# Two stretches of a kernel's own products, repeated behind its last store at other operand distances

## The chip, the cores and the metric

One core of a Trainium2 chip runs the kernel. The time is device microseconds of one execution; the metric is the median over runs.

## The reference

A two-layer decoder trunk on x of 512 tokens by 1024 features, float32, causal. Layer 0 mixes tokens by dilated sliding-window attention (three groups of eight heads, windows 128, 512 and 2048, dilations 1, 4 and 16, joined by their softmax denominators); layer 1 by a recurrent block (RG-LRU). Behind each stands a gated feed-forward part with a causal convolution. Each part is wrapped in two RMS norms and added to the stream:

```
for layer in range(2):
    h = rms_norm(x, norm_mix_pre[layer])
    h = dilated_attention(h) if layer == 0 else rglru(h)
    x = x + rms_norm(h, norm_mix_post[layer])
    h = rms_norm(x, norm_ffn_pre[layer])
    h = (gelu(conv(h @ w_up)[:, :3072]) * conv(h @ w_up)[:, 3072:]) @ w_down
    x = x + rms_norm(h, norm_ffn_post[layer])
```

## The kernel before

Each float32 operand of a large product is split into a high and a low part of type fp32r (`split`: ScalarE copies the high part, VectorE subtracts for the low part), and each product is three: high by high, high by low, low by high (`PASSES`, `mm3`). The moving operand has 512 columns ("long" here) or 256 ("short"); the stationary one has always 128 x 128.

The normed state is kept transposed in one tile, `hT`, high and low part, 2 x 8 x 512 numbers a partition. `new_hT(near)` allocates it with 16 spare numbers and starts the data at the first of them (`near`) or 64 bytes further on:

```
both = htp.tile([P, 2 * KD * S + NEAR], F32R, tag="hT", name=nm("hT"))
at = 0 if near else NEAR
```

In the built program the split weights (`whi`, `wlo`) start at 192 bytes past a multiple of 256, a near `hT` at 128, the other at 192. The state is near in the two feed-forward parts.

In nine of each twelve steps of the feed-forward's first product, and in the strided part of attention, the eight products of a 2 x 2 block scheme are replaced by seven (`seven`, `chain`, line 1040 in before): blocks of 256 columns, whose moving operand is a block of `hT`, or a sum of such blocks from tiles called `T` (`token_sums`), which stand partly on the same residue of 256 bytes as a near `hT` and partly on that of the weights. Between them stand long products: quarters of ordinary tiles, and the second product of the feed-forward (`rows`), both through `mm3` (line 411). In attention the value products (line 1238) stand between, with a weight as moving and `hT` as stationary operand.

The order of all work is written out by hand (the Tile framework's manual schedule), and each engine runs its instructions in that order; waits are set from what reads and writes the same tile. At the end, `norms` with `final` takes the last output tile through the post norm (`rms`, lines 418 to 427), adds it to the stream (line 583, VectorE) and stores it (line 585, queues of SP and ScalarE). `drain` lets what is left run out, and the program ends.

Of the kernel before, what the change touches and what calls it, by code (L numbers as in the profile page):

```python
# [11 lines left out]
F32 = mybir.dt.float32  # L12
# [32 lines left out]
APART, ROUND = 7, 44  # L45
QUARTERS = (28, 30, 31, 32, 34, 35, 36, 37, 38, 39, 40, 41, 42, 43, 45, 49)
HALF = ("s1", "w11", "w12", "a22", "s2", "s3", "s4", "rows", "act")

SHORT_ORDER = [
    ([0, 1], [0, 1, 2]), ([0], [3]), ([2, 3], [0]), ([1], [3]), ([2, 3], [1]), ([2], [2, 3]), ([3], [2, 3]),  # L50
# [33 lines left out]
def kernel(  # L84
# [25 lines left out]
    nc = tc.nc  # L110
# [24 lines left out]
    mm = nc.tensor.matmul  # L135
# [163 lines left out]
    def single(name):  # L299
        return (name[0] if isinstance(name, tuple) else name) in HALF  # L300

# [74 lines left out]
    def tick(length=1):  # L376
        for s in list(sides):
            s[0] -= length
            if s[0] <= 0:
                try:  # L380
                    s[0] = next(s[1])
                except StopIteration:
                    sides.remove(s)
        if not state["hold"]:
            pump(1 if state["even"] or state["live"] >= HALVES - 4 else 2)

    def drain():
        while sides:
            tick()
# [725 lines left out]
    def attention(hT, post, pre):  # L1115
# [50 lines left out]
        def first_values(vs):  # L1166
# [16 lines left out]

            ps = first_transposed(0, 0, range(2))
            warm(WARM - 2)
            take(ids[0], 0)
            first_split(0, 0, ps, range(2, 4))
# [452 lines left out]
    for layer in range(2):  # L1640
# [11 lines left out]
        for half, k in [(1, k) for k in range(0, TAIL, 4)] + [(0, REST[0])] + [(1, k) for k in range(TAIL, 24, 4)]:  # L1652
            rows = ffn_w_down[layer][k * P : (k + 4) * P, half * 512 : half * 512 + 512]
            plan.append(("value", 4, 512, [(rows.rearrange("(k p) c -> p k c", p=P), 512)]))

    def warm(n):

        for _ in range(n):
            mm(warm_ps, one[0][:, :P], one[0], start=True, stop=True)
# [44 lines left out]
    nc.vector.memset(one[0].bitcast(F32), 1.0)  # L1704
    warm_ps = psum("warm")
    warm(WARM)
    root_table()
    hT = attention(hT, (norm_mix_post, 0), (norm_ffn_pre, 0))
    hT = ffn(0, hT, (norm_ffn_post, 0), (norm_mix_pre, 1))
    hT = lru(hT, (norm_mix_post, 1), (norm_ffn_pre, 1))  # L1710
    ffn(1, hT, (norm_ffn_post, 1), None)
    drain()


_INS = [
# [24 lines left out]
```

## Time and profile before

| | |
|---|---|
| median of 2 runs | 1406.99 us (1406.71 to 1407.26) |
| the profiled execution, by its clock | 1406.83 us |
| its span, first to last instruction | 1405.1 us |
| TensorE products | 8741, busy 99% |
| weight loads on TensorE | 8741, busy 89% |
| VectorE, ScalarE, GpSimd busy | 80%, 56%, 16% |
| mean granted TensorE clock | 0.998 |

In the profile a matmul's duration holds the depth of its pipeline; the next one starts long before it ends. The view of windows gives for each stretch (us from the start of the span) its length, the busy time of each engine, the number of records in it, the granted clock, and the share and rate of the DMA engines; records that reach into a window are counted too. The timeline lists start, length, engine, line, operation and tiles, with what ended an idle time in brackets.

### The profile page before, as it was taken

The numbers are of one execution on the slowest core, as the hardware profiler recorded it, in microseconds if no ns is written. First come the engines' busy times: TensorE is split into PE (matmuls) and PEld (weight loads), VectorE is DVE, ScalarE is ACT, GpSimd is POOL, SyncE is SP. The second block draws the span as 40 slices with busy tenths as digits, with TensorE's granted clock in tenths as the row PEclk, the third lists the DMA queues.
The fourth block names the chain that finished last, engine by engine and source line by source line (L and its number), as shares of the span: only waits on it lengthen the run. The fifth ranks groups of instructions, "written<-read, shape, count | busy, mean of one in ns | idle before, by whom it ended". The sixth has DMA issues, their size and how long they took to land.

```text
span 1405.1 us, 23534 instructions
## 1 busy us (share of the span) xinstructions
PE 1395.4 (99%) x8741; PEld 1256.1 (89%) x8741; DVE 1122.2 (80%) x2201; ACT 791.2 (56%) x1646; POOL 225.5 (16%) x344
## 2 busy tenths in 40 slices
PE   9999999999999999999999999999999999999998
PEld 7888999999998898999999888888898999999886
DVE  6576897888866889998888758769789999888843
ACT  7343565454536556666665645589455666666641
POOL 0341342231310102221110001000101212111000
PEclk9999999999999999999999999999999999999999
DMA  7644464656564545766654632431444777664511
GB/s 229 178 141 120 121 182 139 188 149 179 152 213 145 197 157 106 162 153 163 131 138 104 215 130 91 135 121 60 131 145 93 165 150 165 150 136 121 179 54 60
DMA packets 171883, 201.92 MB, mean 144 GB/s; under 512 B 10560, under 2 KB 141080, under 8 KB 171512
## 3 DMA queue, kind: packets, MB, share of 16 engines
q1 hardware_dynamic: 123064, 153.34, 33.9%
q0 software_dynamic: 47856, 46.02, 18.0%
q8 instruction: 69, 1.13, 0.3%
q10 hardware_dynamic: 848, 1.05, 0.2%
q14 instruction: 46, 0.38, 0.1%
HBM read 181.41 MB, written 18.96 MB: 143 GB/s over the span
## 4 chain that ended last, share of the span: by engine, by line
PE 78%; ACT 4%; DVE 4%; issue 1%; DVEq 0%; ACTq 0%
PE ps L1040 34%; PE acc L411 25%; PE ps L411 11%; PE v L1238 6%; DVE xb L1543 1%; DVE wlo L149 1%; PE O L1450 1%; PE S L1384 1%; ACT whi L148 1%; ACT sig L1564 1%; PE tr L505 1%; ACT sig L1583 0%; ACT a L1581 0%; ACT xhi L148 0%; ACT th L1582 0%
## 5 line engine op out<-in xcount | busy, mean ns | idle before, releaser
L149 DVE TENSOR_TENSOR wlo<-raw,whi 128x512 fp32r<-128x512 f32 x620 | 408.8, 686 | 110.5 <-ACT whi L148 108.4
L148 ACT ACTIVATE whi<-raw 128x512 fp32r<-128x512 f32 x620 | 367.1, 625 | 150.8 <-PE acc L411 46.6
L1040 PE MATMUL ps<-T,whi 128*128 128x256 f32 x1664 | 300.6, 281 | 0.7 <-DVE ps L1058 0.7
L411 PE MATMUL ps<-hT,whi 128*128 128x512 f32 (+1 forms) x1088 | 287.6, 353 | 0.0
L1040 PEld LDWEIGHTS ps<-T,whi 128*128 128x128 f32 x1664 | 257.8, 189 | 5.3 <-DVE ps L1058 1.3
L1040 PE MATMUL ps<-T,wlo 128*128 128x256 f32 x832 | 232.9, 280 | 0.0
L1040 PE MATMUL ps<-hT,whi 128*128 128x256 f32 x1248 | 226.0, 280 | 0.0
L411 PEld LDWEIGHTS ps<-hT,whi 128*128 128x128 f32 x1088 | 189.6, 188 | 27.7
L1040 PEld LDWEIGHTS ps<-hT,whi 128*128 128x128 f32 x1248 | 192.9, 189 | 2.6
L411 PE MATMUL ps<-hT,wlo 128*128 128x512 f32 (+1 forms) x544 | 191.5, 352 | 0.0
L1040 PE MATMUL ps<-hT,wlo 128*128 128x256 f32 x624 | 174.7, 280 | 0.0
L185 POOL DMA_DIRECT2D raw<-in_ffn_w_up_dram x72 | 92.8, 1319 | 415.7 <-DVE wlo L149 291.6
L1040 PEld LDWEIGHTS ps<-T,wlo 128*128 128x128 f32 x832 | 158.2, 190 | 0.0
L411 PE MATMUL acc<-whi,ahi 128*128 128x512 f32 x352 | 137.6, 391 | 0.0
L411 PE MATMUL acc<-whi,alo 128*128 128x512 f32 x352 | 137.2, 390 | 0.2
L411 PE MATMUL acc<-wlo,ahi 128*128 128x512 f32 x352 | 137.0, 389 | 0.0
L1040 PEld LDWEIGHTS ps<-hT,wlo 128*128 128x128 f32 x624 | 118.8, 190 | 0.0
L411 PEld LDWEIGHTS ps<-hT,wlo 128*128 128x128 f32 x544 | 102.5, 188 | 14.5
L1049 ACT ACTIVATE part<-ps 128x256 f32<-128x256 f32 x156 | 59.1, 379 | 89.3 <-PE ps L1040 86.7
L1238 PE MATMUL v<-whi,hT 128*128 128x512 f32 x320 | 106.4, 396 | 0.0
L781 DVE SCALAR_TENSOR_TENSOR u<-ps,cols,u 128x511 f32<-128x511 f32 x120 | 89.5, 747 | 5.8 <-ACT u L777 3.7
L777 ACT ACTIVATE u<-ps,cols 128x512 f32<-128x512 f32 x60 | 46.3, 775 | 64.6 <-DVE ps L1053 50.1
(206 smaller groups left out, 2144.8 us busy)
## 6 DMA issues: line engine op xcount, KB each, us to landing
raw<-in_ffn_w_up_dram SPq DMA_DIRECT2D x48, 1024.0 KB
raw<-in_attn_w_qkv_dram SPq DMA_DIRECT2D x67, 512.0 KB
raw<-in_ffn_w_up_dram POOLq DMA_DIRECT2D x72, 256.0 KB, 4.8
raw<-in_ffn_w_down_dram SPq DMA_DIRECT2D x14, 1024.0 KB
dw<-in_ffn_w_down_dram SPq DMA_DIRECT2D x40, 256.0 KB
raw<-in_lru_w_in_dram SPq DMA_DIRECT2D x8, 1024.0 KB
turned<-T POOLq DMA_DIRECT2D x26, 256.0 KB, 2.6
ft<-turned POOLq DMA_DIRECT2D x104, 64.0 KB, 4.7
```

The lines of the kernel that those rows point to most:

```text
L148: nc.scalar.activation(hi, raw, AF.Copy)
L149: nc.vector.tensor_tensor(lo, raw, hi.bitcast(F32), op=ALU.subtract)
L185: nc.gpsimd.dma_start(to, src, accum_op=ALU.add)
L411: mm(dst, l[a], r[b], start=start and n == 0, stop=stop and n == 2)
L505: nc.tensor.transpose(ps[:, k * P : (k + 1) * P], xs[i][:, k * P : (k + 1) * P], ident)
L777: nc.scalar.activation(u, ps, AF.Identity, scale=own[:, j : j + 1], bias=cc[:, 48 + j : 49 + j])
L781: nc.vector.scalar_tensor_tensor(u[:, d:], ps[:, : S - d], wc, u[:, d:], op0=ALU.mult, op1=ALU.add)
L1040: mm(dst, W[wa][0][:, k, :], right[n](ha, k), start=n in (1, 5) and k == q == 0, stop=k == 3 and q == 2, skip_group_check=True,)
L1049: later(1, lambda: nc.scalar.activation(to, dst, AF.Copy))
L1238: mm(bank, hT[a][:, k, t * P : (t + 1) * P], W[b][k % 2][:, 0, :], start=(k, a, b) == (0, 0, 0), stop=(k, a, b) == (KD - 1, 1, 0),)
L1384: mm(ps[:, c], q[hh][:, c], k[hh][:, c], start=True, stop=True)
L1450: mm(po[:, c], vtile(v, r, 2 * gi + hh), pts[gi][:, r], start=gi == 0, stop=gi == 1)
```

## The change

A function `rows_again` is called behind `drain`. It allocates a state tile with `new_hT(True)` (the tile has one buffer, so its readers before must be done), fills the first half A with 1.0 on VectorE and the second half B on GpSimd, takes one PSUM bank, and issues products into it, each a sum of its own that nothing reads.

Two strings name the products. An element such as `sU4W31` is: s for 256 moving columns, l for 512; the moving operand's kind (T, H, U or W) and its slot of 512 numbers in A; the stationary operand's kind, slot in B and block of 128. `FFN_ROW` has 440 elements (368 s, 72 l) and `ATT_ROW` 410 (324 s, 86 l). Kind and size of the elements are in the same order as 440 products of a feed-forward part and 410 of attention (there with 64 products of 128 columns between them, left out here); H stands for `hT`, W for a weight, T and U for sums on the one and the other residue.

Each of the 64 entries of `VARIANTS` runs one string once: F for `FFN_ROW` (46 entries), A for `ATT_ROW` (18). Its three numbers move the operands of kind T, H and U by so many times 16 bytes; those of kind W stand at 12 such units. B starts 16,384 bytes behind A, so that the distance between the starts of two operands, modulo 256 bytes, is 16 times the difference of their numbers. The kernel's own distances are those of ("F", 8, 8, 12) and ("A", 8, 12, 12). The entries are: T = H = 0 to 15 with U at 12, then T = H = U = 0 to 15, then T at 8 and H at 0, 2, 4 ... (and the other way round), and 18 for `ATT_ROW`.

```diff
+VARIANTS = [
+    ("F", 0, 0, 12),
...
+    ("F", 15, 15, 12),
+    ("F", 0, 0, 0),
...
+    ("F", 15, 15, 15),
+    ("F", 8, 0, 12),
...
+    ("F", 0, 8, 12),
...
+    ("A", 8, 12, 12),
...
+    ("A", 13, 13, 13),
+]
...
+    def rows_again():
+
+        A, B = (h.rearrange("p k t -> p (k t)") for h in new_hT(True))
+        nc.vector.memset(A.bitcast(F32), 1.0)
+        nc.gpsimd.memset(B.bitcast(F32), 1.0)
+        ps = psum("again")
+        for kind, t, h, u in VARIANTS:
+            at = {"T": 4 * t, "H": 4 * h, "U": 4 * u, "W": 48}
+            for e in (FFN_ROW if kind == "F" else ATT_ROW).split():
+                n = 256 if e[0] == "s" else 512
+                mv = A[:, 512 * int(e[2]) + at[e[1]] :][:, :n]
+                st = B[:, 512 * int(e[4]) + 128 * int(e[5]) + at[e[3]] :][:, :128]
+                mm(ps[:, :n], st, mv, start=True, stop=True)
...
     ffn(1, hT, (norm_ffn_post, 1), None)
     drain()
+    rows_again()
```

TensorE at the seam, in the program of the change (`acc` is the last output tile's bank, `again` the new one, `hT` the new tile):

```order
L525 MATMUL acc_15331<-whi_15553,ahi_15628 128x512
L525 MATMUL acc_15331<-wlo_15554,ahi_15628 128x512
L525 MATMUL acc_15331<-whi_15553,alo_15629 128x512
L1782 MATMUL again_15888<-hT_15885 128x256 [waits DVE_49,Pool_49]
L1782 MATMUL again_15888<-hT_15885 128x256 x28
L1782 MATMUL again_15888<-hT_15885 128x512 x12
L1782 MATMUL again_15888<-hT_15885 128x256 x12
```

Before, the engine's program ended with the third row. The first added product waits for VectorE and GpSimd, the others for nothing.

VectorE's end in the program of the change (the last two operations on the stream, then the fill of A):

```order
L541 SCALAR_TENSOR_TENSOR s_15866<-s_15867,s_15866 128x1 [waits DVE_49]
L697 SCALAR_TENSOR_TENSOR x_sb_15316<-post_15861,s_15866,x_sb_15316 128x512 [waits DMAHW1_49,DVE_49]
L697 SCALAR_TENSOR_TENSOR x_sb_15316<-post_15862,s_15866,x_sb_15316 128x512
L1773 MEMSET hT_15885 128x4096
L1865 UNCONDITIONAL_BRANCH
```

Before, the branch stood right behind the stream's last operation. The lines above `rows_again` are 114 further down than in the kernel before (583 is 697).

GpSimd's end in the program of the change (its last weight loads, then the fill of B):

```order
L299 DMA raw_14433<-in_ffn_w_up_dram 128x4x128 [waits DVE_49]
L299 DMA raw_14621<-in_ffn_w_up_dram 128x4x128 [waits DMAHW3_49,DMASW6_49,DMASW3_49]
L299 DMA raw_14621<-in_ffn_w_up_dram 128x4x128 [waits DVE_49]
L1774 MEMSET hT_15885 128x4096 [waits PE_49]
L1865 UNCONDITIONAL_BRANCH
```

Before, the branch stood behind the last load. The fill waits for TensorE's last product that reads the tile's earlier content.

More of the change, by code (lines that the diff above doesn't have):

```diff
@@ L47 @@
 HALF = ("s1", "w11", "w12", "a22", "s2", "s3", "s4", "rows", "act")
+FFN_ROW = (
[22 rows of a table added]
+)
+ATT_ROW = (
[21 rows of a table added]
+)
+VARIANTS = [
+    ("F", 0, 0, 12),
+    ("F", 1, 1, 12),
+    ("F", 2, 2, 12),
+    ("F", 3, 3, 12),
+    ("F", 4, 4, 12),
+    ("F", 5, 5, 12),
+    ("F", 6, 6, 12),
+    ("F", 7, 7, 12),
+    ("F", 8, 8, 12),
+    ("F", 9, 9, 12),
+    ("F", 10, 10, 12),
+    ("F", 11, 11, 12),
+    ("F", 12, 12, 12),
+    ("F", 13, 13, 12),
+    ("F", 14, 14, 12),
+    ("F", 15, 15, 12),
+    ("F", 0, 0, 0),
+    ("F", 1, 1, 1),
+    ("F", 2, 2, 2),
+    ("F", 3, 3, 3),
+    ("F", 4, 4, 4),
+    ("F", 5, 5, 5),
+    ("F", 6, 6, 6),
+    ("F", 7, 7, 7),
+    ("F", 8, 8, 8),
+    ("F", 9, 9, 9),
+    ("F", 10, 10, 10),
+    ("F", 11, 11, 11),
+    ("F", 12, 12, 12),
+    ("F", 13, 13, 13),
+    ("F", 14, 14, 14),
+    ("F", 15, 15, 15),
+    ("F", 8, 0, 12),
+    ("F", 8, 2, 12),
+    ("F", 8, 4, 12),
+    ("F", 8, 6, 12),
+    ("F", 8, 10, 12),
+    ("F", 8, 12, 12),
+    ("F", 8, 14, 12),
+    ("F", 0, 8, 12),
+    ("F", 2, 8, 12),
+    ("F", 4, 8, 12),
+    ("F", 6, 8, 12),
+    ("F", 10, 8, 12),
+    ("F", 12, 8, 12),
+    ("F", 14, 8, 12),
+    ("A", 8, 12, 12),
+    ("A", 0, 12, 12),
+    ("A", 4, 12, 12),
+    ("A", 5, 12, 12),
+    ("A", 7, 12, 12),
+    ("A", 9, 12, 12),
+    ("A", 11, 12, 12),
+    ("A", 13, 12, 12),
+    ("A", 8, 8, 12),
+    ("A", 8, 0, 12),
+    ("A", 8, 4, 12),
+    ("A", 8, 11, 12),
+    ("A", 8, 13, 12),
+    ("A", 8, 8, 8),
+    ("A", 0, 0, 0),
+    ("A", 4, 4, 4),
+    ("A", 11, 11, 11),
+    ("A", 13, 13, 13),
+]
 SHORT_ORDER = [
```

43 rows, old and new, of tables (ATT_ROW, FFN_ROW) are left out of this document.

## The prediction

> **What bounds the kernel now.** I read the page first: busy shares, granted clock, the chain that ended last.
>
> ```profile
> span 1405.1 us, 23534 instructions
> PE 1395.4 (99%) x8741; PEld 1256.1 (89%) x8741; DVE 1122.2 (80%) x2201; ACT 791.2 (56%) x1646; POOL 225.5 (16%) x344
> PEclk9999999999999999999999999999999999999999
> PE 78%; ACT 4%; DVE 4%; issue 1%; DVEq 0%; ACTq 0%
> ```
>
> TensorE never rests in 1405 us: 8741 products, full clock. The reader is to see that a product added to this engine has nothing to hide beside. What one costs is its distance to the start of the next, not the "mean ns of one", which includes the pipeline (a 256-column product is listed with 280 ns while another starts each 120 ns). So I take stretches of one kind, and divide their length by the products that start in them. The view of windows gives length and count; the count includes the one to four products that reach in from before.
>
> ```profile
> 498.27:511.97 13.70, 13.70 (x124) 1.00 0.42 149
> 875.64:890.11 14.47, 14.47 (x123) 1.00 0.27 86
> 545.56:553.73 8.17, 8.17 (x74) 1.00 0.53 66
> 511.97:545.56 33.59, 33.59 (x146) 1.00 0.47 114
> 1321.76:1397.84 76.08, 76.08 (x337) 1.00 0.23 83
> ```
>
> Rows one to three are "short" products (256 columns): 120, 120 and 72 start there, so 114.2, 120.6 and 113.5 ns each. Rows four and five are "long" ones (512 columns): 144 and 335, so 233.3 and 227.1 ns. What differs inside a kind is the place of the operands. I took the addresses from the two programs and give the **distance** as start of the moving operand minus start of the stationary one, modulo 256 bytes, where a row of 16-byte units has 16 values. Rows one, three and four have distance 192 (the state that was allocated "near"), rows two and five distance 0. So a distance costs a short product up to 7 ns, in the other order a long one 6 ns. No other distance occurs among such products in this trace; that is the gap of this forecast.
>
> The two stretches that the change repeats stand in this trace too. The string FFN_ROW is the 440 products from 560.03 us on (again at 1094.20), ATT_ROW those from 300.13 on without 64 small products of 128 columns, 16 of which are in the last row here:
>
> ```profile
> 560.03:619.42 59.39, 59.39 (x442) 1.00 0.73 158
> 1094.20:1153.59 59.39, 59.39 (x443) 1.00 0.74 158
> 300.13:365.22 65.09, 65.09 (x475) 1.00 0.61 169
> 334.82:336.52 1.70, 1.70 (x19) 1.00 1.01 323
> ```
>
> FFN_ROW: 59.39 us, twice the same to 0.01. ATT_ROW: 65.09 - 64 x 1.70/16 = 58.3 us.
>
> **The change part by part.** Nothing is removed. Added are one fill on VectorE, one on GpSimd, and on TensorE 46 x 440 + 18 x 410 = 27,620 products with as many weight loads: counted by kind, 22,760 short and 4,860 long.
>
> *The fills and the seam.* The end of the trace, TensorE and VectorE, and the clock:
>
> ```profile
> 1397.84 0.39 PE L411 MATMUL acc<-whi,alo 128*128 128x512 f32 x1
> 1400.30 1.41 DVE L583 SCALAR_TENSOR_TENSOR x_sb<-post,s,x_sb 128x512 f32<-128x512 f32 x2
> 1399.00:1400.00 1.00, 0.00 (x0) 0.00 (x0) 0.96 (x4) 0.28 (x1) 0.00 (x0) 1.00 0.00 0
> 1400.00:1401.00 1.00, 0.00 (x0) 0.00 (x0) 0.93 (x4) 0.00 (x0) 0.00 (x0) 0.88 0.00 0
> 1401.00:1402.00 1.00, 0.00 (x0) 0.00 (x0) 0.71 (x2) 0.00 (x0) 0.00 (x0) 0.50 0.07 27
> L1704 DVE MEMSET one<- x1: 485/485/485, 0.9 to 0.9; 128x512 f32 x1
> 1282.27 1.29 POOL L185 DMA_DIRECT2D raw<-in_ffn_w_up_dram  x1 [7.07 <-DVE wlo L149]
> ```
>
> VectorE's fill stands behind its last two operations, which end at 1401.71. 512 columns took 0.485 us, so 4096 take 0.5 to 3.9 us; I take 3.5, since most of a fill should grow with its columns. GpSimd's last DMA was issued at 1282; its fill waits only for the last reader of the old state tile, which lies before 1321.76, where the run of pure acc products of the fifth row above starts. So it ends some 70 us ahead of the seam and costs nothing; without that cover it would be several us at the same seam. The added products wait for both fills: first start about 1405.2 us into the span. By then TensorE has been idle for 7 us, and the rows show the clock fall from 1.00 to 0.50 some 2.5 us after its last product. Restarting at half:
>
> ```profile
> 1.47 2.50 PE L1659 MATMUL warm<-one 128*128 128x512 f32 x5 [1.47 <-DVE one L1704]
> 6.56 1.31 PE L1176 MATMUL v<-whi,hT 128*128 128x512 f32 x2
> 8.74 1.46 PE L1176 MATMUL v<-whi,hT 128*128 128x512 f32 x4
> ```
>
> At the kernel's start five long products need 2.50 us, some 0.43 apart when the last one's pipeline is taken off, and only near 8.7 us are they dense. Three to seven us at half speed lose half of that: 2 us (1.5 to 3.5). The last store and its wait, which end the span now, lie beside the added products.
>
> *The products.* If each repetition cost what it costs the kernel, the sum is 46 x 59.39 + 18 x 58.3 = 2731.9 + 1049.4 = 3781 us. But the lists of offsets move the operands: counted over all 64 repetitions, 4,476 short products stand at distance 0, 4,112 at 192, and 14,172 at the fourteen others; of the long ones 2,194, 550 and 2,116. For the known ones: at 0 120.6 ns; at 192 what FFN_ROW leaves. Its 42 long ones at 192 and 30 at 0 take 42 x 233.3 + 30 x 227.1 = 16.61 us; of the other 42.78 us its 53 short ones at 0 take 6.39; 315 remain with 36.39, so 115.5 ns (above the 113.5 of pure runs, as kinds alternate). For the unknown distances the ends are 113.5, the densest stretch, and 122, a little over the worst; both known values are equally near, so I take the middle of 115.5 and 120.6: 118.0. Long: 227.1 to 236, taken 230.2.
>
> Short: 4,476 x 120.6 + 4,112 x 115.5 + 14,172 x 118.0 = 539.8 + 474.9 + 1672.3 = 2687.0 us. Long: 2,194 x 227.1 + 550 x 233.3 + 2,116 x 230.2 = 498.3 + 128.3 + 487.1 = 1113.7 us. Together **3801 us**. With the low ends 3730, with the high ones 3870.
>
> The Trainium skill, "TensorE: Matmul & The Clock Gate", section "Back-to-back issue gap", gives a warm product N/2.4 + 2.5 ns, an estimate of 109 ns for 256 columns and 216 for 512. The densest rows here have 113.5 and 227.1, so the trace is 4 to 5% above it even in its best stretches.
>
> *Sum.* 1405.2 + 2 + 3801, + 0.9 for the last product's own pipeline and the closing waits (estimated from 0.39 of a product), + 1.7 outside the span (the profiled execution took 1406.83 by its clock and has a span of 1405.10; the median of the other runs is 1406.99, so the two agree): **5211 us**.
>
> **The rivals.**
>
> *Distance does not matter*, only the sequence does: the repetitions cost what the two stretches cost now. 1405.2 + 2 + 3781 + 2.6 = 5191. For it: both copies of FFN_ROW last 59.39 us, whatever tiles they use, and kinds alternate in them, which may set the pace. Against it: 114.2 and 120.6 ns in long pure runs. The Trainium skill, same page, section "Step-by-step: what each phase is for", says that loading the next tile's weights "doesn't steal SBUF read bandwidth from the running matmul"; by that rule the place of the operands could not matter at all. The two rows differ by 6%, which speaks against it. Chance 0.17.
>
> *Some distances are much worse than those the kernel uses.* The kernel has two of sixteen; if the mean of the others lies as far above 120.6 as that lies above 113.5, at 127.7 (long 239.5), the sum is 539.8 + 474.9 + 1809.8 + 498.3 + 128.3 + 506.8 = 3958, and the time 5368. For it: nothing in the trace bounds the fourteen from above. Against: even the slow distance costs only 7 ns in 120, and both streams move over many units in one product, so that a start is soon left behind. Chance 0.12.
>
> *Each product runs at 109 or 216 ns*, because unread single products with no other engine at work have nothing to disturb them: 22,760 x 0.1092 + 4,860 x 0.2158 = 3534, and 4944 in all. Against it: 0.23 of DMA share in the 227.1 row and 0.47 in the 233.3 row, 0.42 in the 114.2 row and 0.27 in the 120.6 row, so the spacing does not follow the other traffic. Chance 0.04.
>
> *The clock stays low in the stretch.* At half the clock as at the start, about 0.43 us a long product and 0.21 a short: 2090 + 4780 = 6870 us, some 8280 in all. Against: 1393 us at full clock now with a denser mix of engines. Chance 0.02.
>
> *The products are not there* (the other side, not slower). Their sums are never read; if whatever makes the final program dropped them, only VectorE's fill would be left, 3.5 us beside the last store's 3.3 us of waiting: 1407 to 1409. This decides from one condition alone, whether an unread product counts as work. Against it: the built program lists them on TensorE, one bank written over and over. Chance 0.02.
>
> **How the numbers follow.** Forecast 0.63 at 5211, its own range 5140 (all unknown distances at the low ends) to 5280. Half of the heavy case and all of the even-distance case fall near or inside, so I give 5140 to 5290. What a measurement of this kernel can tell from no change is about 2%: faster by more than that 0.005 (no case leads there), within it 0.02 (products dropped), slower 0.975 (all others).
>
> **What would show it.** Two groups at one line on TensorE, 256 columns x22760 and 512 columns x4860; a pause on TensorE from 1398.2 to about 1405 with VectorE's fill as releaser; half clock there and a few us on; then no pause. In windows over single repetitions, those with the kernel's own offsets should take 59.4 and 58.3 us, and the others spread by distance, 57 to 62. GpSimd's fill should stand long before VectorE's. The forecast is wrong if the spread over distances is much wider than the 7 ns of the two known ones, if a pause of the instruction stream appears in 3.8 ms of nothing but products, or if the clock moves.

## The result, and the profile after

The changed kernel takes 5215.7 us (5215.05 to 5216.36, 2 runs) against 1406.99 us before: ratio 3.707, 95% interval 3.691 to 3.723. The forecast was 5211, range 5140 to 5290.

The page after, in the lines that answer those of before: span, busy time, granted clock, chain, and the instruction queue.

```profile
span 5213.2 us, 78777 instructions
PE 5201.0 (100%) x36361; PEld 4853.7 (93%) x36361; DVE 1125.6 (22%) x2202; ACT 791.5 (15%) x1646; POOL 228.8 (4%) x345
PEclk9999999999999999999999999999999999999999
PE 97%; DVE 1%; ACT 1%; DMA 0%; issue 0%; POOL 0%; DVEq 0%; SPq 0%; ACTq 0%
q8 instruction: 284, 4.65, 0.4%
```

TensorE is as dense as before, over a span 3808 us longer, with 27,620 products more. VectorE and GpSimd have one fill more each (about 3.5 us), ScalarE has what it had. Instruction fetch (queue q8) has moved 4.65 MB, and no pause follows from it. The added products by shape, then TensorE's longest wait:

```profile
L1782 PE MATMUL again<-hT 128*128 128x256 f32 x22760 | 2749.1, 280 | 7.9 <-DVE hT L1773 7.9
L1782 PE MATMUL again<-hT 128*128 128x512 f32 x4860 | 1184.6, 393 | 0.0
```

```profile
PE again L1782 <- DVE hT L1773: 7.9, 1, 7.9
```

One wait at the seam, and none in the 3.8 ms behind it. The seam in the timeline (start, length, engine, line, operation), then the windows, whose last column but two is the granted clock:

```profile
1398.24 0.39 PE L525 MATMUL acc<-whi,alo 128*128 128x512 f32 x1
1400.70 1.41 DVE L697 SCALAR_TENSOR_TENSOR x_sb<-post,s,x_sb 128x512 f32<-128x512 f32 x2
1402.92 3.47 DVE L1773 MEMSET hT<- 128x4096 f32 x1 [0.80 <-issue]
1406.54 4.69 PE L1782 MATMUL again<-hT 128*128 128x256 f32 x26 [7.91 <-DVE hT L1773]
1312.73 3.54 POOL L1774 MEMSET hT<- 128x4096 f32 x1 [28.76 <-PE ps L1154]
```

```profile
1402.00:1404.00 2.00, 0.00 (x0) 0.00 (x0) 1.20 (x2) 0.00 (x0) 0.00 (x0) 0.70 0.70 262
1404.00:1406.00 2.00, 0.00 (x0) 0.00 (x0) 2.00 (x1) 0.00 (x0) 0.00 (x0) 0.50 0.00 0
1408.00:1410.00 2.00, 2.00 (x12) 2.00 (x12) 0.00 (x0) 0.00 (x0) 0.00 (x0) 0.59 0.00 0
1410.00:1412.00 2.00, 2.00 (x17) 1.91 (x16) 0.00 (x0) 0.00 (x0) 0.00 (x0) 1.00 0.00 0
```

GpSimd's fill lay at 1312.7, long before. The first added product started at 1406.54; at half clock 13 short products follow each other at 213 ns, then the others at 118.

Single repetitions in the view of windows. Each window runs from the first start of a repetition to the first start of the next, taken from the trace; its length is the repetition's time, and a busy time of the same size says that there is no pause in it. In order: ("F", 8, 8, 12), the kernel's own offsets; ("F", 3, 3, 3), the best F; ("A", 8, 12, 12), the kernel's own; ("A", 8, 8, 8), the best A; ("A", 4, 4, 4), the worst A.

```profile
1889.30:1948.48 59.18, 59.18 (x443) 1.00 0.00 1
2550.94:2609.38 58.44, 58.44 (x442) 1.00 0.00 1
4168.16:4226.01 57.85, 57.85 (x413) 1.00 0.00 1
4922.50:4979.01 56.51, 56.51 (x412) 1.00 0.00 1
5037.23:5096.06 58.83, 58.83 (x412) 1.00 0.00 1
```

The repetition with the kernel's own offsets has 59.18 us where the kernel's stretch has 59.39. Start by start the two agree within 3 ns in all but 5 of the 440 products. The 0.21 us are three holds, 189, 158 and 222 ns between starts where the repetition has 113 to 118; both copies of the stretch in the kernel have them at the same places, and what causes them stays open. So but for these holds neither the other engines, nor DMA at 0.73 of its share, nor the values (all 1.0 here), nor the PSUM bank, nor whether a sum is kept, sets the pace.

The same comparison tells the distance from the place of a single operand. In the kernel the weights start at 192 and a near `hT` at 128 bytes past a multiple of 256. The new tile's data start at 128 too, so that in this repetition the operands of kind W, at 12 units, start at 64 and those of kind H, at 8 units, at 0: all places are others by 128 bytes, the distances are the same, and so are the spacings. From the starts in the trace, all 64 repetitions together: short products take 119.5 ns in the mean at distance 0, 115.7 at 192 bytes, 118.2 at the fourteen others; long ones 228.6, 233.1 and 231.9.

### The profile page after: what moved, and what is told of

Same layout as the page of the kernel before. It is cut to its first block, busy times and chain, and to the rows that moved or that the text cites. A ratio compares the mean times of both kernels' runs of the same rounds, so it can differ in the third digit from the quotient of the medians.

```text
span 5213.2 us, 78777 instructions
## 1 busy us (share of the span) xinstructions
PE 5201.0 (100%) x36361; PEld 4853.7 (93%) x36361; DVE 1125.6 (22%) x2202; ACT 791.5 (15%) x1646; POOL 228.8 (4%) x345
## 3 DMA queue, kind: packets, MB, share of 16 engines
q8 instruction: 284, 4.65, 0.4%
## 4 chain that ended last, share of the span: by engine, by line
PE 97%; DVE 1%; ACT 1%; DMA 0%; issue 0%; POOL 0%; DVEq 0%; SPq 0%; ACTq 0%
PE again L1782 73%; PE ps L1154 10%; PE acc L525 7%; PE ps L525 5%; PE v L1352 2%; PE v L1290 0%; DVE xb L1657 0%; DVE wlo L263 0%; PE O L1564 0%; PE S L1498 0%; PE S L1446 0%; ACT whi L262 0%; ACT sig L1678 0%; PE tr L619 0%; PE O L525 0%
## 5 line engine op out<-in xcount | busy, mean ns | idle before, releaser
L1782 PE MATMUL again<-hT 128*128 128x256 f32 (+1 forms) x27620 | 3805.7, 300 | 7.9 <-DVE hT L1773 7.9
L1782 PEld LDWEIGHTS again<-hT 128*128 128x128 f32 x27620 | 3597.9, 189 | 215.8 <-issue 8.3
```

What stands on the lines that cost most here:

```text
L1782: mm(ps[:, :n], st, mv, start=True, stop=True)
```

## The experiments

Two theories stood against each other: the place of the operands sets the pace; or the sequence does, and the place is nothing. Later a third one joined: what stands ahead of a run also counts (its **entry**). Runs e1, e2, e4 and e6 are the changed kernel with other products behind the last store, e3 has the same products and moves a fill. Each of the five ran once; the readings rest on the spacings inside its trace more than on its total.

**All repetitions at the kernel's own offsets.**

```diff
-VARIANTS = [
...
-]
+VARIANTS = [("F", 8, 8, 12)] * 46 + [("A", 8, 12, 12)] * 18
```

> All 64 repetitions at the kernel's own offsets, otherwise the change unaltered. Theory 'distance': 46 x 59.18 + 18 x 57.85 = 3763.6 us by the changed kernel's own two windows against 3805.6 now, so about 42 us less: 5174 us (the first repetition 1.5 us longer from the restart). Rival 'distance does not matter, only the sequence': no change, 5216. Also: every repetition behind the first should be equal to the nanosecond of its own string.

Measured: 5176.5 us, 39 less than the change. Same sequence, same counts, other distances: the place counts, on average 1.4 ns a product. The 45 repetitions of FFN_ROW behind the first are equal to 1 ns in 59,180; the second and the third:

```profile
1468.58:1527.76 59.18, 59.18 (x443) 1.00 0.00 1
1527.76:1586.94 59.18, 59.18 (x443) 1.00 0.00 1
```

The expected 5174 was missed by 2.5 us: the first repetition took 62.01, 2.8 longer than the others and not 1.5, because full clock came back 5.9 us behind its start, where the change had 3.1; and the repetitions of ATT_ROW took 57.89 where I had 57.85.

**Pure runs.** The strings are replaced by

```diff
+VARIANTS = [(entry, d) for entry in (12, 8) for d in range(16)] + [(None, d) for d in range(16)]
...
+        for entry, d in VARIANTS:
+            if entry is not None:
+                run("l", entry, 12)
+                run("s", d, 360)
+            else:
+                run("l", d, 120)
```

> The two strings are replaced by pure runs. First 16 runs of 360 short products, one for each distance of 0 to 15 units of 16 bytes (moving start: 0 to 15 units; stationary at 12), each behind 12 long products at distance 0; the same again, each behind 12 long products at distance 192 bytes (12 units); then 16 runs of 120 long products. Theory 'a distance has its price, and nothing else matters': a run at a given distance costs the same in both passes, near what the changed kernel shows in the mean: 119.5 ns at 0, 115.7 at 12, 114.1 at 7, 117 to 120 at the others; long 227 at 0, 233 at 12. Theory 'the start of the run sets a rhythm that is kept': at 12 units the run behind long ones at distance 0 keeps 117.8 ns and the one behind long ones at 12 keeps 113.4 for all 360 products, as in the kernel's own stretches; 4.4 ns x 360 = 1.6 us between the two passes; other distances may show the same. Rival 'sequence, not distance': in pure runs all sixteen cost alike, near 117.

Mean nanoseconds from start to start, by distance in units of 16 bytes (the stationary operand stands at 12 units, so a moving start of d is the distance d - 12, modulo 16); short runs behind twelve long products at distance 0 (a) and at 192 bytes (b), long runs (c), from the starts in the trace:

| units | 0 | 1 | 2 | 3 | 4 | 5 | 6 | 7 | 8 | 9 | 10 | 11 | 12 | 13 | 14 | 15 |
|---|---|---|---|---|---|---|---|---|---|---|---|---|---|---|---|---|
| a | 120.0 | 118.7 | 116.7 | 118.3 | 117.8 | 120.0 | 120.0 | 113.4 | 120.0 | 116.7 | 118.7 | 119.2 | 117.8 | 119.2 | 118.3 | 117.2 |
| b | 120.0 | 113.3 | 117.8 | 118.3 | 117.8 | 120.0 | 120.0 | 113.4 | 118.7 | 118.6 | 118.7 | 119.3 | 117.8 | 119.2 | 118.3 | 117.1 |
| c | 227.0 | 231.6 | 233.4 | 233.3 | 228.9 | 231.1 | 233.4 | 231.1 | 232.4 | 233.2 | 234.3 | 233.3 | 233.3 | 234.6 | 233.3 | 226.7 |

The windows of units 7, 9, 1 in pass a and then b (359 intervals each), and of long ones at 13 and 15 units (119 intervals):

```profile
1547.03:1587.75 40.72, 40.72 (x360) 1.00 0.00 1
1636.58:1678.46 41.88, 41.88 (x361) 1.00 0.00 1
1999.40:2042.01 42.61, 42.61 (x361) 1.00 0.00 1
...
2272.19:2312.91 40.72, 40.72 (x360) 1.00 0.01 1
2361.33:2403.93 42.60, 42.60 (x361) 1.00 0.00 1
2725.36:2766.05 40.69, 40.69 (x361) 1.00 0.01 1
...
3107.68:3135.60 27.92, 27.92 (x121) 1.00 0.00 1
3163.83:3190.81 26.98, 26.98 (x121) 1.00 0.00 1
```

The rival of pure sequence falls: sixteen runs, 113.4 to 120.0. The theory of one price falls too, at four distances (1, 2, 8, 9), where the entry decides: 118.7 or 113.3 at one unit. At 192 bytes (12 units) my expectation failed: both runs kept 117.8, none the 113.4 that the kernel shows at the same distance. Row c has one run at each distance and one entry, so it doesn't tell which of its differences come from the entry.

**Modulo 256.** All moving operands moved together by a further m units, then H alone through sixteen places:

```diff
+    ("F", t + m, h + m, u + m, m)
+    for t, h, u in ((8, 8, 12), (3, 3, 12), (12, 12, 12))
+    for m in (0, 8, 16, 32, 64)
+] + [("F", 8, h, 12, 0) for h in range(16)]
...
+                up = 4 * m if e[1] == "W" else 0
+                mv = A[:, 512 * int(e[2]) + at[e[1]] + up :][:, :n]
```

> FFN_ROW alone. Three sets of offsets (T, H, U) = (8, 8, 12), (3, 3, 12), (12, 12, 12), each with all moving operands, those of kind W too, moved by a further 0, 128, 256, 512 and 1024 bytes. Theory 'only the distance modulo 256 bytes counts': 256, 512 and 1024 leave a repetition as it is (59.18, 59.0, 60.6 us, to 0.05), 128 changes it by 0.3 us or more. Rival 'the true distance or the bits above count': 512 or 1024 differ from 0 by 0.3 us or more. Then FFN_ROW with T at 8, U at 12 and H at 0 to 15: H at 3 (112 bytes before the next multiple, distance 7 units) should be near the best, by 0.1 to 0.4 us below 59.18, if the mean prices of the changed kernel (114.1 at 7 units, 115.7 at 12) add up.

Set (8, 8, 12) moved by 256, 128 and 1024 bytes, set (3, 3, 12) by 128 and 256:

```profile
1527.00:1586.18 59.18, 59.18 (x442) 1.00 0.00 1
1466.99:1527.00 60.01, 60.01 (x443) 1.00 0.00 1
1645.36:1704.54 59.18, 59.18 (x442) 1.00 0.00 1
1763.55:1823.53 59.98, 59.98 (x443) 1.00 0.00 1
1823.53:1882.47 58.94, 58.94 (x442) 1.00 0.00 1
```

256, 512 and 1024 bytes leave a repetition as it was, with one exception by 0.06 us (58.95 for 59.01, unexplained); 128 bytes cost 0.8 to 1.0, in the third set they gain 0.2. The stationary operands stayed where they were: with the shift of both operands by 128 bytes above, which changed nothing, this says that the difference of the two places counts. The second expectation failed: with H alone at 7 units the repetition takes 59.71, 0.53 more than at 12, though pure runs at 7 units are among the fastest. Of sixteen places for H, the kernel's own was the best by 0.49 us. Mean prices by distance do not add up. That each change of distance between blocks has a price of its own would explain it; it was not measured by itself.

**Both fills on GpSimd**, which is idle:

```diff
-        nc.vector.memset(A.bitcast(F32), 1.0)
+        nc.gpsimd.memset(A.bitcast(F32), 1.0)
```

> The change with both fills on GpSimd, where they lie under the last products. If the seam costs what the trace shows (8.3 us of pause and 1.5 us of half clock): the first added product starts right behind the last of the kernel, no half clock, time 5215.7 - 9.8 = 5206. If the clock falls anyway or the pause has another cause (the bank, a barrier): within 2 us of 5215.7.

```profile
1397.88 0.40 PE L525 MATMUL acc<-whi,alo 128*128 128x512 f32 x1
1398.11 2.65 PE L1782 MATMUL again<-hT 128*128 128x256 f32 x21
1400.00:1402.00 2.00, 2.00 (x17) 1.00 0.02 7
```

5204.97 us, 10.7 below the median of the change and 10.1 below its profiled execution; 9.8 were expected. The first added product starts 8.43 us sooner, and from first to last start it takes 1.65 us less. There is no pause, and the spacings are 117 to 122 ns from the first short product on, so the clock did not fall: the seam was VectorE's fill and what it set off.

**The entry.** Only what stands ahead of a run at 192 bytes changes (l and s, offset with stationary at 12, count):

```diff
+    "l12x12 s8x360 s12x12 s8x360 l8x12 s8x120 l12x6 s8x120 l8x12 s8x120 s12x12 s8x120 l12x12 s8x120 "
+    "s3x12 s8x120 s12x12 s3x120 l12x12 s3x120 l12x12 s13x360 s12x12 s13x360 l8x12 s13x120 l12x6 s13x120"
```

> The two strings are replaced by 25 runs, all pure, one behind the other; what changes is only what stands ahead of a run of short products at distance 192 bytes. Theory 'two rhythms, the entry chooses': behind 12 long at 0: 117.8 ns, kept for 360; behind 12 short at 0: 113.4 ns, kept for 360; then 12 long at 192 and 120 short: still 113.4 (long ones at 192 carry the rhythm over); then 6 long at 0 and 120 short: 117.8; 12 long at 192 and 120 short: still 117.8; 12 short at 0: 113.4 again. Rival 'the run finds its own pace': every run at 192 settles at the same 117.8 after a few products, and the 113.4 of the kernel has another cause (its tiles' higher address bits). At 112 bytes (7 units) 113.4 behind any entry. At 16 bytes (1 unit), behind long ones at 0 118.7, behind the others 113.3 or 118.7.

The first seven runs at 192 bytes; ahead of them stand long at 0, short at 0, long at 192, long at 0, long at 192, short at 0, long at 0:

```profile
1411.35:1453.75 42.40, 42.40 (x362) 1.00 0.00 1
1455.18:1496.00 40.82, 40.82 (x363) 1.00 0.00 1
1498.79:1512.40 13.61, 13.61 (x122) 1.00 0.00 1
1513.77:1527.91 14.14, 14.14 (x122) 1.00 0.00 1
1530.71:1544.32 13.61, 13.61 (x122) 1.00 0.01 1
1545.74:1559.36 13.62, 13.62 (x123) 1.00 0.00 1
1562.09:1576.23 14.14, 14.14 (x122) 1.00 0.01 1
```

The seven take 117.8 ns, 113.4, 113.4, 117.8, 113.4, 113.5 and 117.8, each kept to the end of its run: two rhythms at one distance, chosen by the entry. One of seven was not as expected: the fifth, behind long ones at 192 that followed slow short ones, should have stayed slow and was fast. In pass b above long ones at 192 led to the slow rhythm. The long ones have two rhythms as well (231 and 236 in turn, or 233), and which leads where I cannot say beforehand: 231 and 236 in turn stood ahead of the 117.8 of pass b, and of the 113.4 of the third run here. At 112 bytes both runs settled at 113.3 or so, after up to 11 slower spacings. At 16 bytes the runs behind long and behind short products at distance 0 took 118.7, the one behind long ones at 192 bytes 113.4, as expected.

The kernel's own sequence shows the same. In the repetition with its offsets, 99 of the 315 short products at 192 bytes stand behind long ones at distance 0 and take 117.8 in the mean; the other 216 stand behind short ones at 0 or long ones at 192 and take 113.5 to 114.2 block by block.

**Put to use: the kernel before with another order** (nothing repeated). In the feed-forward's cycle the short blocks behind a fill of long ones at 0 run at 117.8 until a block at distance 0 has passed. The fill is moved to places 3 and 4 of the cycle, and that block (step 4) to the place right behind it:

```diff
-AT = {1: 0, 5: 1, 2: 2, 6: 4, 3: 5, 7: 8, 4: 13}
+AT = {1: 0, 5: 1, 2: 2, 6: 6, 3: 7, 7: 8, 4: 15}
-        free = [CYCLE * c + r for c in range(n) for r in ((6, 7, 9) if c < 3 or c > 8 else (6, 7))][2:] + [end, end + 1]
+        free = [CYCLE * c + r for c in range(n) for r in ((3, 4, 9) if c < 3 or c > 8 else (3, 4))][2:] + [end, end + 1]
```

> The kernel before, nothing repeated, with another order inside the cycle of ten of the feed-forward: the fills (long products at distance 0, L411) move from places 6 and 7 to 3 and 4, and the block whose T stands at distance 0 (step 4) from 13 to 15, so that it is the first short block behind the fills; steps 6 and 3 move two places back. Theory 'entry chooses': the some 48 short products per cycle that ran at 117.8 behind long ones at 0 run at 113.4, 0.2 us a cycle, about 22 cycles of 36 have such a fill: 4 to 7 us less, 1400 to 1403, if no new wait arises. Rival 'distance has one price': 1407, or more by what the new order makes TensorE wait.

1407.42 against 1407.40, ratio 1.0002 (0.9993 to 1.0011): 4 to 7 us were expected, and there is no gain. The trace shows why: of the 4955 spacings between two short products 2353 lie at 112 to 115 ns where before 1567 did, and all of them sum to 582.2 us for 586.0, so 3.9 us are saved there. But a wait that the kernel before does not have stands behind the first product of both feed-forward parts (in all, times, longest); the two add 3.2 us to the spacings of the long products:

```profile
PE acc L411 <- DVE u L781: 3.1, 2, 1.5
790.72 0.47 PE L411 MATMUL acc<-whi,ahi 128*128 128x512 f32 x1 [1.55 <-DVE u L781]
```

The last blocks are two places later, and the next product waits until VectorE has read its bank.

The other order, fills at 5 and 6, steps 6 and 3 at 3 and 4, step 4 at 17:

> As the run ahead, with the fills at places 5 and 6, steps 6 and 3 one place earlier and step 4 at 17, behind the fills of the next cycle. Same expectation: 1400 to 1403 by the theory, less of it if step 4, which is now later by four places, holds its buffers long enough to make others wait; 1407 by the rival.

1409.88 us, ratio 1.0017 (1.0008 to 1.0027): no gain but 2.5 us more. 1946 of its spacings lie at 112 to 115 ns, more than before too, yet they sum to 588.9 us, as new waits stand between short products; the two longest spacings, 1.49 us each, make 2.7 us of it:

```profile
PE ps L1040 <- ACT part L1049: 2.4, 2, 1.2
```

**The first order, with the old places in the last cycle** (and step 4 at its old place in the last but one):

```diff
+LAST_AT = {1: 0, 5: 1, 2: 2, 6: 4, 3: 5, 7: 8, 4: 13}
+    def places(c, n):
+        if c == n - 1:
+            return LAST_AT
+        return {**AT, 4: 13} if c == n - 2 else AT
...
-                steps.update((CYCLE * n + AT[p], f(p)) for p in AT)
+                at = places(n, 2 * len(SEVEN))
+                steps.update((CYCLE * n + at[p], f(p)) for p in at)
```

> The order of e8_order, but with the places of the kernel before in the last cycle of each feed-forward part, so that the first block of the next product (acc, L411) finds its PSUM bank freed as early as before. In e8_order TensorE waited there twice, 3.1 us in all, behind VectorE's last tap (u, L781), while its 4955 short products were 3.9 us faster. If those are two separate things: the waits go, most of the 3.9 us stays, 1403 to 1404.5 us. If the gain is always given back (a later engine sets the pace): 1407.

1403.47 us against 1407.03, ratio 0.9973 (0.9962 to 0.9984): a quarter of a per cent, small but clear, as its highest time (1404.21) is below the lowest of before (1406.65). The wait on the bank is not in its list of waits. From first to last start TensorE takes 3.36 us less: the spacings between short products give 3.76, a wait ahead of a short product at 209 us that is longer than before takes 0.6 back, and no other class changes by more than 0.25. Of the short spacings 2332 lie at 112 to 115 ns, 765 more than before; at the 4.4 ns between the two rhythms these are 3.4 us. So the gain is that of the rhythm.

## Why the prediction was right, point by point

- **The first start** was put at 1405.2, measured 1406.54. The fill took 3.47 us for 3.5; with the 512 columns in 0.485 us this is 0.83 ns a column, so that a fill did grow with its columns. Missing were the 0.80 us of "issue" ahead of the fill, 0.4 by which the kernel's own end came later, and 0.15 from the fill's end to the first start.
- **The clock** cost 2 us by estimate. The first 26 products took 4.53 us from start to start; at 118 ns they would take 3.07, thus 1.5. The moved fill took the half clock away, and the products behind it came out 1.65 us shorter. The prediction read the half clock at the kernel's start from spacings of 0.43 us. The column of the clock has 1.00 there, but the clock records of that trace begin only 8.1 us in, so the spacings are the evidence and not the column.
- **The products**: 3801 forecast; from first to last start 3805.4, less the 1.5 of the clock 3803.9. Some of that closeness is luck: the class at distance 0, short, came out 5 us lower than forecast, the long classes 7 us higher. By class: short at 0 120.6 forecast and 119.5 measured, at 192 115.5 and 115.7, elsewhere 118.0 and 118.2; long 227.1 and 228.6, 233.3 and 233.1, 230.2 and 231.9.
- **The unknown distances** were the weakest step: a middle between two known ones, with a worst end of 122. The pure runs of short products show that no distance is slower than 120.0, so that 0, which the trace had, was among the worst already, and 7 units, at 113.4, ties with the best. The mean of the fourteen is 118.2 in pass a. That the middle of two hit it was luck. So was that it lay between the known ends, as far as the trace before goes: nothing in that trace bounded the fourteen, as the rival of much worse distances said.
- **115.5 at 192**, above the 113.5 of pure runs, was put down to alternating kinds. That is right in effect, but the working took each distance to have one price, and this is not so: 2000 of the 4112 short products at 192 bytes took 116 to 125 ns, the others 113 to 115, and what stands ahead decides it. The pure stretches of the forecast happened to stand in the rhythm of 113 to 114 ns.
- **Distance does not matter** (5191): falls by the 39 us of the first experiment and by the pure runs. The sentence of the Trainium skill, "TensorE: Matmul & The Clock Gate", section "Step-by-step: what each phase is for", that a weight load "doesn't steal SBUF read bandwidth from the running matmul", would leave the place of the operands without effect, and here the spacing goes from 113.4 to 120.0 ns with nothing but the distance changed. Whether the load takes bandwidth from the running product or something else delays one of them was not seen and stays open. So does which load it is, as in a run of one distance a product stands at the same distance from its own stationary operand and from the next one's.
- **Much worse distances** (5368), **109 and 216 ns a product** (4944), **half clock** and **dropped products** are all refuted by the table, the counts and the clock of the profile after.
- **Single repetitions** were to take 57 to 62 us; they took 56.5 to 61.3, the latter the first, with the clock's restart. Those with the kernel's own offsets were to take 59.4 and 58.3; they took 59.18, as the three holds are missing, and 57.85.

## What to carry to other kernels

On a saturated TensorE, price added products by start-to-start spacing in a pure stretch of the same trace, by shape, operand distance modulo 256 bytes and what stands ahead; the listed durations are about twice as long (280 ns for 118). Where stretches of the very sequence stand in the trace, their length is the best price, since it repeats to the nanosecond. A saving on the saturated engine is real only when the next buffer comes free as early as before: 3.9 us were gained and 3.2 of them lost again to one wait in each feed-forward part, until the last cycle kept its old order.

## What the runs showed of the hardware that was not expected

- In the pure runs, products of 256 fp32r columns with a weight load each follow each other after 113.3 to 120.0 ns in the mean at full clock, by the distance of their operands in 16 steps of 16 bytes, and products of 512 columns after 226.7 to 234.6. A further 256, 512 or 1024 bytes change nothing. At half clock short products show 213 to 214 ns.
- At several distances there are two stable rhythms (113.3 or 118.7 at 16 bytes; 113.4 or 117.8 at 192), kept for as long as was tried, 360 products. What stands ahead chooses between them, but the long products' own rhythm has a part in it that is not resolved.
- Spacing is otherwise blind: FFN_ROW at equal offsets took 59.18 us 45 times with 1 ns of spread, and inside the kernel, beside DMA and the other engines and with other values, the same sequence kept its spacings but for three holds of 0.21 us in all.
